# Decaying the scan's states in the copy out of PSUM, and two buffers for the inversion

## The chip, the cores and the metric

The kernel runs on one core of a Trainium2 chip. The metric is the time of one execution on the device in microseconds, as a median over several runs. The engines are TensorE (PE, with its weight loads as PEld), VectorE (DVE), ScalarE (ACT), GpSimd (POOL), and SyncE (SP), which issues the DMA transfers. Each engine works through its own queue in order.

## What is computed

The reference is a two-layer encoder. Each layer has a feed-forward half-step, a token mixer, and a second half-step, with a layer norm behind each. Layer 0 mixes by neighbourhood attention, layer 1 by a bidirectional RWKV-7 scan over 512 tokens, with 16 heads of 64 channels. The change concerns the scan alone, which in the reference reads:

```python
def step(state, inp):
    r_t, w_t, k_t, v_t, a_t, b_t = inp
    sa = jnp.einsum('zbhij,zbhj->zbhi', state, a_t)
    state = state * w_t[..., None, :] + sa[..., None] * b_t[..., None, :] + v_t[..., None] * k_t[..., None, :]
    return state, jnp.einsum('zbhij,zbhj->zbhi', state, r_t)

_, ys = lax.scan(step, jnp.zeros((2, B, H, N, N), f32), xs)
```

`z` is the direction. All of it is float32.

## The kernel before

The kernel does not step token by token. It cuts the 512 tokens into 8 chunks of 64 and takes two heads at a time, a pair; there are 8 pairs. Partitions 0 to 63 and 64 to 127 (`HALF`) hold the two directions or the two heads. For each pair there is preparation work and then a chain of 8 steps, one per chunk, in which the state of a chunk is made from that of the one before.

Preparation of a pair, by name of its function:

- `load` and `front` make the decayed a~, r~ (tile `ar`) and b~, k~ (tile `bk`) of each direction. The decay over a whole chunk is kept twice: `pe`, and `pc` with the two heads side by side.
- `grams` multiplies `bk` with `ar` for each chunk (PE, bank `g`), masks the products into `xs` (DVE), copies blocks of them to `qd` and `qc` (ACT), and has SP write parts to `az` and `xs`. At its end it multiplies `bk` by `pe`, L1067.
- `tails` transposes `bk` on PE and copies it into `tb`.
- `turn` makes `pd`, a diagonal matrix of the chunk decays for every chunk and head, L1114, and lays the values `v` out in `vt`.
- `invert` inverts the 32 x 32 triangular blocks. A DVE transpose (L1135) makes `qs` from `qd`, a DMA (L1137) sets `zs` to unit matrices, and POOL does 31 pairs of a product (L1143) and a sum (L1145). `inverted` transposes `zs` back (L1155), writes the blocks into `az` by eight DMAs (L1160), and transposes once more (L1162), into the memory of `qs`. `merge` combines the blocks on PE (L1174, L1181) and ACT.

The chain (`chain`) does for each step: products of `xs` with the state `vt` (L1202 and L1206), an ACT copy to `wr` (L1203), products with the inverse in `az` (L1215), two ACT copies into `vt` (L1216, L1217), and then the next state in bank `m`: the diagonal `pd` times the old state (L1212) plus `tb` times `vt` (L1221). Two DVE copies (L1223), one per direction, bring it to `vt` of the next chunk. `outputs` adds products to the pair's result, and `finish` and `gate` normalise and gate it.

The order on PE, ACT and DVE is written out by hand: `slot(n)` runs the chain of pair n beside the preparation of pairs n+1 to n+3 and the finish of pair n-1, and the string `SEQ[n]` says which thread goes on next, each up to its next `yield`. There c is the chain, k `inverted`, i `invert`, j `merge`, g0 and g1 `grams`, f0 and f1 `front`, t0 and t1 `tails`, n `turn`, x `finish`, e `gate`, v `values`, b `bonus`, d `outputs`, l `load`. Slots -2 and -1 have only preparation (and the thread r, projections that are computed on the side); slots 1 to 5 use the string of slot 0; slots 6 and 7 have their own, with the thread o (part of the output projection). POOL's and SP's queues follow the order in which the instructions are written. A tile's buffers are given again in turn, and a new use waits for the last readers of the buffer; `zs`, `qs` and `tm` have one, `qd`, `qc`, `ar`, `bk`, `vt` have two.

Of the kernel before, what the change touches and what calls it, by code (L numbers as in the profile page):

```python
# [10 lines left out]
F32 = mybir.dt.float32  # L11
# [3 lines left out]
AF = mybir.ActivationFunctionType  # L15
# [42 lines left out]
}  # L58
SEQ = {
# [782 lines left out]
class Scan:  # L842


    def __init__(self, k, pool, dram, consts, a2, w_r, w_v, w_out):
        self.k, self.nc, self.pool, self.dram, self.a2, self.w_r, self.w_v, self.w_out = k, k.nc, pool, dram, a2, w_r, w_v, w_out
        nc = self.nc
        self.tri = pool.tile([P, 2, P], F32, name="tri")
        self.mask = pool.tile([P, 2, 2, CH], F32, name="mask")
        self.onesb = pool.tile([P, P], F32, name="onesb")  # L850
        self.eye = consts["eye"]
        self.ah = pool.tile([P, 2, S], F32R, name="ah")
        self.xv = pool.tile([P, ND, S], F32, name="xv")
        self.consts = consts
        self.units = [(pool.tile([P, 2, 4, 2, CH], F32, name=f"xs{i}"), pool.tile([P, 2, 4, CH], F32, name=f"tb{i}"))
                      for i in range(NBUF)]


        self.az = [pool.tile([P, 2, NU, CH], F32, name=f"az{i}") for i in range(3)]
        self.eye64 = pool.tile([P, CH], F32, name="eye64")  # L860
        nc.vector.tensor_tensor(self.eye64, k.ident[:, A], k.ident[:, B], ALU.add)
        for i in range(2):
            self.clear(i)
        self.free = list(range(NBUF))
        self.taken, self.st, self.py = {}, {}, {}
# [57 lines left out]
    def run(self):  # L923
        with self.k.tc.manual_schedule(engines=MANUAL_SCAN):
            raw = self.tile("e", [P, S], 2)
            for dst, src in ((raw, self.dram["ah"]), (self.tri, self.consts["tri"])):
                self.nc.sync.dma_start(dst, src)
            list(self.load(0))
            self.k.split(self.ah[:, 0, :], self.ah[:, 1, :], raw)
            list(self.front(0, 0))  # L930
            for n in ("mask", "onesb"):
                self.nc.sync.dma_start(getattr(self, n), self.consts[n])
            self.rs, self.out = self.receptances(), self.outs()
            for n in range(-2, HEADS // 2):
                self.slot(n)
            list(self.finish(HEADS // 2 - 1))
            list(self.gate(HEADS // 2 - 1))
# [18 lines left out]
    def load(self, hp):  # L956

        k, nc, tile_ = self.k, self.nc, self.tile
        p = self.st[hp] = Pair()
        p.k, p.iv = (tile_(n, [P, S], 2) for n in ("k", "iv"))  # L960
        nc.sync.dma_start(p.k, self.dram["rkv"][1][:, hp, :])
        for h in range(2):
            nc.sync.dma_start(p.iv[HALF[h]], self.dram["iv"][2 * hp + h : 2 * hp + h + 1, :].broadcast_to([CH, S]))
        raw = tile_("a2r", [P, 2, P])
        nc.sync.dma_start(raw, self.a2[:, :, hp * P : (hp + 1) * P])
        yield
        p.a2u = self.pool.tile([P, 2, 2, P], F32R, name="a2u", tag="a2u", bufs=1)
        k.split(p.a2u[:, 0], p.a2u[:, 1], raw)
        p.pc = tile_("pc", [P, NC, 2], 4)
        p.qd = tile_("qd", [P, NU, 32], 2)  # L970
        p.qc = tile_("qc", [P, NU, 32], 2)
        p.az = self.az[hp % 3]
        p.units, p.ar, p.bk, p.pe = [], [], [], []
        yield

    def front(self, hp, z):
# [31 lines left out]
        nc.vector.scalar_tensor_tensor(a1, k1, k.col(C_NKK, hp), e1, ALU.mult, ALU.mult)  # L1008
        nc.vector.tensor_scalar(a0, k0, k.col(C_NKK, hp), None, ALU.mult)
        end = 0 if z else CH - 1  # L1010
        pe = tile_("pe", [P, NC, 1], 3)
        ends = ec[:, way, end : end + 1]
        nc.scalar.activation(pe, ends, AF.Copy)
        for h in range(2):
            nc.scalar.activation(p.pc[HALF[z], :, h : h + 1], ends[HALF[h]], AF.Copy)
        yield
# [10 lines left out]
        nc.vector.scalar_tensor_tensor(bt, chunks(th), 1.0, chunks(e2), ALU.add, ALU.mult)  # L1027
        p.ar.append(ar)
        p.bk.append(bk)
        p.pe.append(pe)  # L1030
        if z:
            yield
            nc.vector.tensor_tensor(kz, p.kz, kz, ALU.add)
# [3 lines left out]
    def grams(self, hp, z):  # L1037

        k, nc = self.k, self.nc
        p = self.st[hp]  # L1040
        ar, bk = p.ar[z], p.bk[z]
        own, other, r = HALF[z], HALF[1 - z], z * CH
        for q in range(2):
            x, az = self.take(hp, z, q)[0], p.az[:, :, z * NC + q * 4 : z * NC + q * 4 + 4]
            ss, us = slice(q * 4, q * 4 + 4), slice(z * NC + q * 4, z * NC + q * 4 + 4)
            pgs = [k.bank("g") for _ in HALF]

            for j in range(4):
                for h, hs in enumerate(HALF):
                    nc.tensor.matmul(pgs[h][:, j * P : (j + 1) * P], flat(bk[hs, q * 4 + j]), flat(ar[hs, q * 4 + j]),  # L1050
                                     start=True, stop=True)

            mask = self.mask[:, z].rearrange("p (o a) t -> p o a t", o=1).broadcast_to([P, 4, 2, CH])
            for h in range(2):
                nc.vector.tensor_tensor(x[:, h], pgs[h].rearrange("p (u a t) -> p u a t", u=4, a=2), mask, ALU.mult)
            yield
            for h, hs in enumerate(HALF):
                for d in range(2):
                    nc.scalar.activation(p.qd[h * 64 + d * 32 : h * 64 + d * 32 + 32, us, :],
                                         x[r + d * 32 : r + d * 32 + 32, h, :, 0, d * 32 : d * 32 + 32], AF.Copy)  # L1060
                nc.scalar.activation(p.qc[h * 64 : h * 64 + 32, us, :], x[r : r + 32, h, :, 0, 32:64], AF.Copy)
                nc.sync.dma_start(az[own, h], x[own, h, :, 1, :])
                nc.sync.dma_start(x[own, h], ar[hs, ss])
                yield

        bke = bk.rearrange("p s a t -> p s (a t)")
        nc.vector.tensor_tensor(bke, bke, p.pe[z].broadcast_to([P, NC, 2 * CH]), ALU.mult)  # L1067
        yield

    def tails(self, hp, z):  # L1070

# [37 lines left out]
    def turn(self, hp):  # L1109

        k, nc, tile_ = self.k, self.nc, self.tile
        p = self.st[hp]
        p.pd = tile_("pd", [P, NC, 2, CH], 2)
        nc.vector.tensor_tensor(p.pd, self.eye64.rearrange("p (a b t) -> p a b t", a=1, b=1).broadcast_to([P, NC, 2, CH]),  # L1114
                                p.pc.rearrange("p s (h o) -> p s h o", o=1).broadcast_to([P, NC, 2, CH]), ALU.mult)
        p.vt = tile_("vt", [P, NC, 2, 2, CH], 2)
        for z, zs in enumerate(HALF):
            nc.vector.memset(p.vt[zs, 0, z], 0.0)
# [3 lines left out]
        for z in range(2):  # L1122
# [4 lines left out]
                nc.scalar.activation(p.vt[HALF[1 - z], j::2, z], pv[HALF[j]].rearrange("p (t h i) -> p t h i", t=NT, h=2), AF.Copy)  # L1127
            yield

    def invert(self, hp):  # L1130

        nc, tile_ = self.nc, self.tile
        p = self.st[hp]
        qs = tile_("qs", [P, 32, 32])
        nc.vector.transpose(flat(qs), p.qd.rearrange("p u (t o) -> p t u o", o=1).broadcast_to([P, 32, NU, 2]))  # L1135
        zs = tile_("zs", [P, 32, 16])
        nc.sync.dma_start(zs, self.eye)  # L1137
        for s in range(31, 0, -1):
            c0 = s // 2
            n = 16 - c0  # L1140
# [8 lines left out]
    def inverted(self, hp):  # L1149
# [6 lines left out]
        for h in range(2):  # L1156
            for d in range(2):
                for z in range(2):
                    r, us = HALF[1 - z].start + d * 32, slice(z * NC, z * NC + NC)
                    nc.sync.dma_start(p.az[r : r + 32, h, us, d * 32 : d * 32 + 32], p.zc[h * 64 + d * 32 : h * 64 + d * 32 + 32, us])  # L1160
        yield
        nc.vector.transpose(flat(p.zt), flat(p.zc))  # L1162
        yield
# [24 lines left out]
    def chain(self, hp):  # L1188
# [6 lines left out]
        for s in range(NC):  # L1195
# [11 lines left out]
            yield  # L1207
            if 0 < s < NC - 1:

                for z, h in zh:  # L1210
                    zs = HALF[z]
                    nc.tensor.matmul(pm[zs, h], p.pd[zs, s, h], vt[zs, s, z, h], start=h == 0, stop=False)  # L1212
            for z, h in zh:
                ws = HALF[1 - z]
                nc.tensor.matmul(pw[HALF[z], 1, h], az[z][ws, h, s, :], wr[ws, h], start=True, stop=True)  # L1215
# [3 lines left out]
            if s < NC - 1:  # L1219
                for z, h in zh:  # L1220
                    nc.tensor.matmul(pm[HALF[z], h], tb[z][:, h, s % 4, :], vt[:, s, z, h], start=s + h == 0, stop=h == 1)  # L1221
                for z, zs in enumerate(HALF):
                    nc.vector.tensor_copy(vt[zs, s + 1, z], pm[zs])  # L1223
                yield

    def outputs(self, hp):
# [230 lines left out]
```

## Time and profile before

| | us |
|---|---|
| median of 3 runs | 2376.36 (2374.26 to 2377.40) |
| profiled execution, its own time | 2376.21 |
| its span, first to last instruction | 2374.3 |
| PE busy / DVE busy / ACT busy / POOL busy | 2215.5 / 1141.9 / 984.1 / 1439.5 |

Busy time counts each moment once in which an instruction of the engine is in flight. PE's busy time is an upper view: matmul records overlap. A float32 matmul appears as two records. The scan lies between about 1493 and 1960 us of the span; the rest is projections, attention and feed-forward work that the change does not touch.

### The profile page before, as it was taken

The numbers are of one execution on the slowest core, as the hardware profiler recorded it, in microseconds if no ns is written. First come the engines' busy times: TensorE is split into PE (matmuls) and PEld (weight loads), VectorE is DVE, ScalarE is ACT, GpSimd is POOL, SyncE is SP. The second block draws the span as 40 slices with busy tenths as digits, with TensorE's granted clock in tenths as the row PEclk, the third lists the DMA queues.
The fourth block names the chain that finished last, engine by engine and source line by source line (L and its number), as shares of the span: only waits on it lengthen the run. The fifth ranks groups of instructions, "written<-read, shape, count | busy, mean of one in ns | idle before, by whom it ended". The sixth has DMA issues, their size and how long they took to land.

```text
span 2374.3 us, 34996 instructions
## 1 busy us (share of the span) xinstructions
PE 2215.5 (93%) x13664; PEld 1746.6 (74%) x13664; DVE 1141.9 (48%) x1575; ACT 984.1 (41%) x1728; POOL 1439.5 (61%) x1231
## 2 busy tenths in 40 slices
PE   8999999999999999999999789799998884999998
PEld 7888878777888888888888665456666553888886
DVE  2333366355523335723335696346877546233336
ACT  3333344466433333533333435346676423233334
POOL 7787744544658785778775433136756605477863
PEclk9999999999999999999999889799999996999999
DMA  6444453421534446344445325843443516344453
GB/s 201 146 146 139 133 186 116 134 74 49 168 98 139 144 136 232 112 134 143 141 139 193 118 82 188 266 126 103 115 120 100 155 60 212 98 139 145 146 172 116
DMA packets 351361, 330.38 MB, mean 139 GB/s; under 512 B 48554, under 2 KB 277546, under 8 KB 351196
## 3 DMA queue, kind: packets, MB, share of 16 engines
q1 hardware_dynamic: 351196, 328.15, 43.9%
q8 instruction: 107, 1.75, 0.3%
q14 instruction: 58, 0.48, 0.1%
HBM read 263.05 MB, written 48.53 MB: 131 GB/s over the span
## 4 chain that ended last, share of the span: by engine, by line
PE 74%; DVE 12%; DMA 5%; issue 3%; POOL 3%; ACT 2%; SPq 1%; DVEq 0%; ACTq 0%; POOLq 0%
PE bank L201 15%; PE bank L203 15%; PE bank L202 15%; PE bank L668 12%; PE bank L239 3%; DVE x L306 2%; PE a L1091 1%; DVE x L373 1%; POOL zs L1145 1%; POOL tm L1143 1%; DVE tmp L303 1%; DVE w L197 1%; PE y L904 1%; PE g L1263 1%; PE bank L793 1%
## 5 line engine op out<-in xcount | busy, mean ns | idle before, releaser
L197 POOL TENSOR_TENSOR w<-raw,w 128x1024 fp32r<-128x1024 f32 (+2 forms) x203 | 502.4, 2475 | 319.6 <-ACT w L196 319.5
L201 PE MATMUL bank<-xT,w 128*128 128x512 f32 x1416 | 554.0, 392 | 0.0
L202 PE MATMUL bank<-xT,w 128*128 128x512 f32 x1416 | 552.0, 390 | 0.0
L203 PE MATMUL bank<-xT,w 128*128 128x512 f32 x1416 | 551.8, 390 | 0.0
L196 ACT ACTIVATE w<-raw 128x1024 fp32r<-128x1024 f32 (+1 forms) x207 | 218.7, 1057 | 339.2 <-POOL ts L639 141.9
L347 DVE SCALAR_TENSOR_TENSOR ar<-bank,tmp 128x512 f32<-128x512 f32 x88 | 60.9, 692 | 587.3 <-PE bank L203 572.4
L201 PEld LDWEIGHTS bank<-xT,w 128*128 128x128 f32 x1416 | 266.2, 188 | 55.8
L203 PEld LDWEIGHTS bank<-xT,w 128*128 128x128 f32 x1416 | 266.4, 188 | 55.5
L202 PEld LDWEIGHTS bank<-xT,w 128*128 128x128 f32 x1416 | 266.5, 188 | 54.4
L668 PE MATMUL bank<-w,ring 128*128 128x512 f32 x864 | 202.8, 393 | 11.1 <-DVE w L197 10.2
L668 PEld LDWEIGHTS bank<-w,ring 128*128 128x128 f32 x864 | 162.6, 189 | 48.6 <-DVE w L197 13.2
L1143 POOL TENSOR_TENSOR tm<-qs,zs 128x126 f32<-128x126 f32 (+22 forms) x248 | 105.0, 424 | 138.6 <-DMA zs<-in_eye_dram 85.3
L668 PE MATMUL bank<-wx,an 128*128 128x512 f32 x792 | 187.3, 389 | 0.0
L668 PEld LDWEIGHTS bank<-wx,an 128*128 128x128 f32 x792 | 148.7, 188 | 30.9
L197 POOL TENSOR_TENSOR wx<-ra,wx 128x512 fp32r<-128x512 f32 x132 | 168.3, 1302 | 0.0
L197 DVE TENSOR_TENSOR ring<-ar,ring 128x1024 fp32r<-128x1024 f32 x44 | 130.7, 2970 | 72.8 <-ACT ring L196 72.7
L345 ACT ACTIVATE tmp<-bank 128x512 f32<-128x512 f32 x88 | 52.6, 597 | 238.0 <-PE bank L203 238.0
L1145 POOL TENSOR_TENSOR zs<-zs,tm 128x126 f32<-128x126 f32 (+22 forms) x248 | 114.3, 461 | 19.4
L196 ACT ACTIVATE wx<-ra 128x512 fp32r<-128x512 f32 x132 | 83.1, 632 | 91.5 <-PE bank L668 68.0
L197 POOL TENSOR_TENSOR w<-late,w 128x1024 fp32r<-128x1024 f32 x28 | 70.2, 2507 | 79.3 <-ACT w L196 72.4
L639 POOL TENSOR_TENSOR ts<-ra 128x512 f32<-128x512 f32 x44 | 57.7, 1311 | 87.5 <-DMA raw<-in_rw_out_dram 78.5
L201 PE MATMUL bank<-xT,ring 128*128 128x256 f32 (+1 forms) x352 | 102.2, 305 | 8.6 <-ACT xT L196 6.4
(280 smaller groups left out, 3886.7 us busy)
## 6 DMA issues: line engine op xcount, KB each, us to landing
raw<-in_ffn_w_in_dram SPq DMA_DIRECT2D x176, 512.0 KB, 3.7
ra<-in_ffn_w_out_dram SPq DMA_DIRECT2D x44, 1024.0 KB, 4.9
late<-d_late SPq DMA_DIRECT2D x30, 512.0 KB, 5.3
late<-in_ffn_w_out_dram SPq DMA_DIRECT2D x28, 512.0 KB, 4.3
raw<-in_w_qkv_dram SPq DMA_DIRECT2D x24, 512.0 KB, 3.7
d_late<-ts SPq DMA_DIRECT2D x44, 256.0 KB, 3.3
d_late<-ra SPq DMA_DIRECT2D x44, 256.0 KB, 2.0
xs<-ar SPq DMA_DIRECT2D x64, 128.0 KB, 2.3
```

The source lines that it names most:

```text
L196: self.nc.scalar.activation(h, raw, AF.Copy)
L197: (eng or self.nc.vector).tensor_tensor(l, raw, h.bitcast(F32), ALU.subtract)
L201: nc.tensor.matmul(out, wh, xh, start=start, stop=False)
L202: nc.tensor.matmul(out, wh, xl, start=False, stop=False)
L203: nc.tensor.matmul(out, wl, xh, start=False, stop=stop)
L239: nc.tensor.matmul(acc[t, h], a, u[:, i, h * 512 : (h + 1) * 512], start=first and n == 0, stop=last and n == 2)
L345: nc.scalar.activation(s, pg, AF.Silu)
L347: nc.vector.scalar_tensor_tensor(raw[:, 3:7:3] if j else raw[:, 0:8:7], halves_of(pu), 0.5, halves_of(s), ALU.mult, ALU.mult)
L639: nc.gpsimd.tensor_tensor(t3, r[:, 1, 1], r[:, 0, 1], ALU.subtract)
L668: self.nc.tensor.matmul(acc, lhs, u[:, i], start=bool(first) and m == 0, stop=last and m == 2, skip_group_check=more)
L1143: nc.gpsimd.tensor_tensor(tv, qs[:, s, 0:s].rearrange("p (a o) -> p a o", o=1).broadcast_to([P, s, n]), zs[:, s : s + 1, c0:].broadcast_to ...
L1145: nc.gpsimd.tensor_tensor(zs[:, 0:s, c0:], zs[:, 0:s, c0:], tv, ALU.add)
```

## The change

The diff has three parts. The first: b~ and k~ and the old state are no longer decayed one by one. `pe`, `pd` and the unit matrix `eye64` go; the old state is added to bank `m` by a product with the unit matrix, for both heads in one instruction; and the copy of `m` to the next state becomes a product with `pc`, a number per partition and head.

The second: `qs` and `zs` have two buffers, and the unit matrices are loaded by `unit`, twice before the slots and then from `inverted` for the pair two further on.

The third: the strings of slots -2, -1 and 0 are new.

```diff
 SEQ = {
...
-    0: "f1 n x x c c c n c g0 f1 c x c d c g0 f1 v f1 c g0 g0 c c d v c f1 v l x c v f1 v c c g0 x c d l f0 x c g1 e "
...
+    0: "c f1 x f1 v c n c f1 f1 v c g0 c c d f1 c n c d g0 l v c c g0 c x f1 g0 c x x v n x t0 v c c l c d g0 f0 c "
...
-        self.eye64 = pool.tile([P, CH], F32, name="eye64")
-        nc.vector.tensor_tensor(self.eye64, k.ident[:, A], k.ident[:, B], ALU.add)
...
+            self.zs = []
+            for _ in range(2):
+                self.unit()
...
-        pe = tile_("pe", [P, NC, 1], 3)
         ends = ec[:, way, end : end + 1]
-        nc.scalar.activation(pe, ends, AF.Copy)
...
-        bke = bk.rearrange("p s a t -> p s (a t)")
-        nc.vector.tensor_tensor(bke, bke, p.pe[z].broadcast_to([P, NC, 2 * CH]), ALU.mult)
-        yield
...
-        p.pd = tile_("pd", [P, NC, 2, CH], 2)
-        nc.vector.tensor_tensor(p.pd, self.eye64.rearrange("p (a b t) -> p a b t", a=1, b=1).broadcast_to([P, NC, 2, CH]),
-                                p.pc.rearrange("p s (h o) -> p s h o", o=1).broadcast_to([P, NC, 2, CH]), ALU.mult)
...
+    def unit(self):
+        self.zs.append(self.tile("zs", [P, 32, 16], 2))
+        self.nc.sync.dma_start(self.zs[-1], self.eye)
+
...
-        qs = tile_("qs", [P, 32, 32])
+        qs = tile_("qs", [P, 32, 32], 2)
...
-        zs = tile_("zs", [P, 32, 16])
-        nc.sync.dma_start(zs, self.eye)
+        zs = self.zs.pop(0)
...
+        if hp + 2 < HEADS // 2:
+            self.unit()
         yield
...
-                for z, h in zh:
-                    zs = HALF[z]
-                    nc.tensor.matmul(pm[zs, h], p.pd[zs, s, h], vt[zs, s, z, h], start=h == 0, stop=False)
+                for z, zs in enumerate(HALF):
+                    nc.tensor.matmul(pm[zs], k.ident[zs, zs], vt[zs, s, z], start=True, stop=False)
...
-                    nc.vector.tensor_copy(vt[zs, s + 1, z], pm[zs])
+                    nc.vector.tensor_tensor(vt[zs, s + 1, z], pm[zs], p.pc[zs, s].rearrange("p (h o) -> p h o", o=1).broadcast_to([CH, 2, CH]),
+                                            ALU.mult)
```

How the instructions move on DVE, in a steady slot, from the last state copy ahead of the three transposes. Before the change (`vt<-m` is the state's copy, `qd<-zs` and the first `qs<-qd` belong to `inverted`, the second `qs<-qd` to `invert`, `bk` and `e` to `front`, `bon` to `bonus`):

```order
L1223 COPY vt<-m 64x128 x2
L1008 SCALAR_TENSOR_TENSOR ar<-k,cols,e 128x8x63
L1009 TENSOR_SCALAR ar<-k,cols 128x8
L1155 STREAM_TRANSPOSE qd<-zs 128x16x16x2
L1162 STREAM_TRANSPOSE qs<-qd 128x512
L1135 STREAM_TRANSPOSE qs<-qd 128x1024
L1017 TENSOR_TENSOR ar<-r,e 128x8x64
L1019 SCALAR_TENSOR_TENSOR iv<-k,cols,iv 128x512
L1067 TENSOR_TENSOR bk<-bk,pe 128x1024
L1223 COPY vt<-m 64x128 x2
```

The same place after the change:

```order
L1218 TENSOR_TENSOR vt<-m,pc 64x128 x2
L1149 STREAM_TRANSPOSE qd<-zs 128x16x16x2
L1158 STREAM_TRANSPOSE qs<-qd 128x512
L1130 STREAM_TRANSPOSE qs<-qd 128x1024
L1094 SCALAR_TENSOR_TENSOR kz<-r,cols,kz 128x512
L1218 TENSOR_TENSOR vt<-m,pc 64x128 x2
```

Between the two state copies stand four instructions instead of eight; the two `qs<-qd` follow one another as before, but write different buffers now.

On DVE again, the rows that follow, up to the first state copy of the next slot. Before (`pd` is the diagonal, `sm` and `yt` belong to `finish`):

```order
L1105 TENSOR_TENSOR bon<-a,v 128x512
L1023 TENSOR_TENSOR kz<-kz,k 128x512
L1024 TENSOR_TENSOR bk<-kz,e_13349 128x8x64
L1026 TENSOR_TENSOR e_13349<-iv,e_13349 128x512
L1027 SCALAR_TENSOR_TENSOR bk<-th,e_13349 128x8x64
L1114 TENSOR_TENSOR pd<-eye_10778,pc 128x1024
L1118 MEMSET vt 64x128 x2
L1281 TENSOR_REDUCE sm<-yt 128x8
```

After the change, behind the state copy that ends the rows shown above:

```order
L1009 SCALAR_TENSOR_TENSOR ar<-k,cols,e 128x8x63
L1010 TENSOR_SCALAR ar<-k,cols 128x8
L1016 TENSOR_TENSOR ar<-r,e 128x8x64
L1018 SCALAR_TENSOR_TENSOR iv<-k,cols,iv 128x512
L1022 TENSOR_TENSOR kz<-kz,k 128x512
L1023 TENSOR_TENSOR bk<-kz,e_13293 128x8x64
L1025 TENSOR_TENSOR e_13293<-iv,e_13293 128x512
L1026 SCALAR_TENSOR_TENSOR bk<-th,e_13293 128x8x64
L1099 TENSOR_TENSOR bon<-a,v 128x512
L1109 MEMSET vt 64x128 x2
```

The whole front of one direction now stands here, the diagonal is gone, and the reduction of `finish` has left this stretch: it comes after the second state copy of the slot.

## Rows read from the trace of the kernel before

**Rows 1.** Busy table by stretches of the scan; (x) counts, then clock, DMA
```profile
core 0: us, PE busy (x) PEld busy (x) DVE busy (x) ACT busy (x) POOL busy (x), PEclk, DMA share, GB/s
1493.00:1610.60 117.60, 97.53 (x509) 53.94 (x508) 50.13 (x77) 48.07 (x118) 36.76 (x93) 0.87 0.63 190
1610.60:1649.30 38.70, 37.83 (x619) 27.13 (x618) 28.42 (x50) 28.41 (x80) 18.90 (x40) 1.00 0.47 126
...
1694.20:1738.80 44.60, 40.15 (x623) 29.08 (x622) 34.94 (x68) 29.31 (x82) 29.36 (x64) 0.92 0.43 116
...
1872.00:1921.70 49.70, 44.53 (x556) 24.28 (x554) 15.65 (x41) 14.29 (x39) 22.57 (x62) 0.97 0.30 95
```

**Rows 2.** Waits: engine, line, waited for, us in total, times, longest us
```profile
POOL tm L1143 <- DMA zs<-in_eye_dram: 85.3, 5, 37.2
```

**Rows 3.** Chain that ended last, 1682 to 1694: start us, us, what
```profile
1682.46 1.08 DVE qd L1155
...
1689.89 3.36 DMA zs<-in_eye_dram
...
1693.42 0.55 POOL tm L1143
```

**Rows 4.** Timeline of DVE and POOL: start us, us, instruction, [idle before it <-releaser]
```profile
1683.57 0.71 DVE L1162 STREAM_TRANSPOSE qs<-qd 128x512 f32<-128x512 f32 x1
1685.72 1.25 DVE L1135 STREAM_TRANSPOSE qs<-qd 128x1024 f32<-128x1024 f32 x1 [1.44 <-PE p L1174]
...
1693.42 0.54 POOL L1143 TENSOR_TENSOR tm<-qs,zs 128x31 f32<-128x31 f32 x1 [10.99 <-DMA zs<-in_eye_dram]
1693.78 1.26 DVE L1114 TENSOR_TENSOR pd<-eye,pc 128x1024 f32<-128x1024 f32 x1
1694.03 1.13 POOL L1145 TENSOR_TENSOR zs<-zs,tm 128x31 f32<-128x31 f32 x1
...
1695.55 0.26 POOL L1145 TENSOR_TENSOR zs<-zs,tm 128x30 f32<-128x30 f32 x1
```

**Rows 5.** Busy table by stretches, two inversions from first to last instruction
```profile
1693.40:1727.20 33.80, 29.80 (x390) 21.64 (x388) 25.91 (x55) 19.66 (x59) 29.00 (x62) 0.90 0.42 118
1876.10:1903.40 27.30, 24.76 (x252) 13.13 (x253) 8.13 (x25) 6.81 (x19) 22.52 (x62) 0.94 0.32 116
```

**Rows 6.** Groups by line, 1493 to 1960: busy us, mean ns | idle before
```profile
L1055 DVE TENSOR_TENSOR xs<-g,mask 128x512 f32<-128x512 f32 x64 | 41.2, 686 | 18.4 <-PE g L1050 17.8
...
L1223 DVE COPY vt<-m 64x128 f32<-64x128 f32 x112 | 32.2, 288 | 60.0 <-PE m L1221 57.2
...
L1067 DVE TENSOR_TENSOR bk<-bk,pe 128x1024 f32<-128x1024 f32 x16 | 20.3, 1270 | 0.0
...
L1114 DVE TENSOR_TENSOR pd<-eye,pc 128x1024 f32<-128x1024 f32 x8 | 9.9, 1244 | 0.0
...
L182 DVE TENSOR_TENSOR sm<-sm 128x8 f32<-128x8 f32 x24 | 5.0, 208 | 0.8
```

**Rows 7.** Chain that ended last, 1719 to 1762: start us, us, what
```profile
1719.74 0.38 PE m L1212 x8
...
1740.07 0.70 DVE sm L1281
1740.79 0.18 DVE sm L1282
1741.00 0.77 DVE yt L1283
1741.79 0.63 ACT yh L1285
...
1742.64 0.81 PE c L1215 x7
...
1745.12 2.06 PE g L1050 x16
...
1760.99 1.09 PE g L1050 x16
```

More of the change, by code (lines that the diff above doesn't have):

```diff
@@ L972, in load @@
         p.az = self.az[hp % 3]
-        p.units, p.ar, p.bk, p.pe = [], [], [], []
+        p.units, p.ar, p.bk = [], [], []
         yield
@@ L1029, in front @@
         p.bk.append(bk)
-        p.pe.append(pe)
         if z:
```

12 rows, old and new, of the table SEQ are left out of this document.

## Prediction

> **What bounds the kernel now.** I read the busy table by stretches of the scan first, then the list of waits, then the chain that ended last, then single stretches of the timeline. The scan works on eight head pairs in slots; a slot is taken from the first state matmul (L1202) of one pair to that of the next. The startup before slot 0 takes 117.6 us, slot 0 38.7 us, slot 2 44.6 us, and slots 1 to 5 together 1872.0 - 1649.3 = 222.7 us, 44.5 us each [rows 1]. No engine fills a steady slot: DVE is busy 34.9 of 44.6 us, ACT 29.3, POOL 29.4, and PE's records cover 40.2 us but overlap, at a mean granted clock of only 0.92 of full speed [rows 1]; PE has slack. What fills the slot must be loops of dependent work, and I see two of nearly the same length.
>
> The first is POOL's. The inversion of a pair runs from 1693.4 to 1727.2, 33.8 us [rows 5]. Then POOL stands still: the next one starts only when a fresh unit matrix has landed, which is the longest sum among POOL's waits, 85.3 us in five cases [rows 2]. In the chain one sees why: the single buffer is free when DVE has transposed it (from 1682.46), its reload is issued behind eight other writes, takes 3.36 us from 1689.89, and POOL goes on at 1693.42 [rows 3], idle for 10.99 us [rows 4]. 33.8 + 11.0 is 44.8 us, a slot.
>
> The second loop is that of the engines that work in order: the order puts some fifteen wide DVE instructions from the transposes to the first state copy of the next slot, the longest such stretch. The chain there goes through the first part of the previous pair's normalisation (0.70, 0.18 and 0.77 us on DVE), a 0.63 us square on ACT, and only then ACT can copy the step's product, for which PE's L1215 waits (1742.64) [rows 7]. PE idles meanwhile, and what it does next runs at 1.2 GHz: sixteen L1050 records take 2.06 us there and 1.09 us at 2.4 GHz later in the slot [rows 7].
>
> **The change, part by part.**
>
> The unit matrix. With two buffers and a load issued when the previous pair's inversion is read, a whole slot ahead, the load leaves POOL's loop. A second buffer of the other tile, qs, lets the transpose that starts an inversion (L1135, now L1130) follow directly on the two that end the one before; until now it waited for PE's L1174, which read the same buffer (1.44 us) [rows 4]. What is left between two inversions is three transposes one behind the other, 1.08 + 0.71 + 1.25 us [rows 3, 4], and about 0.3 us each way between the engines: 3.6 us instead of 11. DVE's wait for POOL stands where it stood; behind it are queued the transposes, step 6's state copy and the next front, and PE's L1170 waits for the second transpose, so what POOL is late, all of them are late.
>
> POOL's speed. The inversion took 27.3 us where DVE was busy 8.1 us of it and 33.8 us where DVE was busy 25.9 us [rows 5]. The rows show why: one POOL instruction took 1.13 us while DVE's L1114 ran, and its like took 0.26 us just after [rows 4]. L1114 reads two SBUF tiles, as L1067 does. Both go: three instructions per slot, 2 x 1.27 + 1.24 = 3.8 us [rows 6]. If each holds POOL for about two thirds of its length where it meets an inversion, that is some 1.3 us of 33.8; but of the 11 us in which DVE worked without disturbing POOL only 3.6 us are left, which gives most of that back. I take 33.5 us. POOL's loop is then 33.5 + 3.6 = 37.1 us, a floor for the steady slot.
>
> DVE's removed work. Sixteen L1067 (20.3 us) and eight L1114 (9.9 us) leave DVE [rows 6]. All of L1114 and one of a slot's two L1067 stand in that long stretch; the other stands ahead of a state copy. So the loop of the in-order engines loses up to 3.8 us: 44.5 - 3.8 = 40.7 us. The new order also puts the normalisation's first part behind step 1's state copy, so that 0.70 + 0.18 + 0.77 + 0.63 = 2.3 us go from the first step [rows 7]; ACT has a few copies and exponentials there in exchange, so I count half: 39.5 us. PE's stretch at 1.2 GHz costs up to 1 us per sixteen such records [rows 7] and may go with the stall; I count 0.5 us: 39.0 us. That is above POOL's floor, so I take 39.0 us for slots 1 to 5, with 37.1 and 42.5 as ends (the latter if only half of the 3.8 us is on the path).
>
> The state's copy. It becomes a product with the decay, read from PSUM and a broadcast column: 112 instructions, 14 in a slot, two on the path of each step. The copy takes 0.288 us [rows 6]. No row has the new form; the nearest are the product out of PSUM with 512 columns (0.686 us) and a product of 8 columns (0.208 us) [rows 6]. A straight line between them gives 0.322 us for 128 columns, 0.034 more. The ends are 0.208 (below the copy, -9.0 us over 112) and 0.686 us (+44.6 us). I take the line: 112 x 0.034 = 3.8 us, of which I count 1.4 us, since in steady slots it lies beside POOL's loop and only in three of eight slots (0, 6, 7) nothing of POOL binds.
> The Trainium skill (VectorE: DVE Perf Modes, The perf-mode tier table) gives a copy out of PSUM up to twice the rate of a product of two tensors. By that rule and the page's own cycles the product would be an estimated 64 / 0.96 = 67 ns dearer, 7.5 us in all and 3.7 us above the sum below; the trace speaks against a copy at twice the rate, as the line between two product rows comes within 0.034 us of it.
>
> PE. Four 64-column products with the diagonal per step (0.38 us for eight records [rows 7]) become two of 128 columns with the unit matrix. Two such products are four records, a quarter of L1050's sixteen in 1.09 us [rows 7], 0.27 us. It is 0.1 us in 48 steps, 5 us if PE were on the path; PE has slack, so nothing, with -5 as the end below. ACT loses sixteen tiny copies: nothing, as ACT isn't full. The transposes of b~ and k~ no longer wait for L1067, which is in the 3.8 us.
>
> Queues. SP issues as many unit loads as before; two of them move to the start, ahead of the projections' loads. In the worst case they delay them by 2 x 3.36 us [rows 3]; PE has the second front's matmuls in front of those, so I take 0, with +4. The startup loses two L1067 per pair on DVE too: -4 at best. Slots 6 and 7 keep their order and are mostly PE's; the last inversion starts earlier, and the tails end earlier: I take -1.5 us, from 0 to -5.
>
> The sum: slots 1 to 5, 222.7 - 5 x 39.0 = 27.7 us gained; slot 0, which has no normalisation to move, half of its 3.8 us, 1.9 us; the end 1.5 us; the state's product costs 1.4 us; startup 0. Together 29.7 us. The profiled execution took 2376.21 us (its span and 1.9 us around it), 0.15 us from the median of the runs. The forecast is 2376.2 - 29.7 = 2346.5 us.
>
> **Rivals.**
>
> 1. The in-order loop hardly shortens: the new order trades one stall for another (on ACT, step 0 now has the y copy, two exponentials and a reversal between the two copies of the chain). Then the steady slot is 41 to 43 us: 222.7 - 5 x 42 = 12.7 us, with the rest of the sum about 14.7 us gained, 2361 us (2356 to 2369). For it: both loops are equal now, so freeing one alone gives nothing. Against: most of the removed DVE work stands in DVE's longest stretch.
>
> 2. POOL's floor is reached, and startup and end give their best: 222.7 - 5 x 37.1 = 37.2 us, with slot 0, the startup and the end some 43 us, 2333 us (2328 to 2338). For it: slot 0, with the work that goes still in it and no normalisation, ran in 38.7 us [rows 1]. Against: every wait would have to fall into place.
>
> 3. POOL is held for the whole of every DVE instruction with two SBUF inputs. By the code eighteen wide ones remain in a steady slot, 13.9 us at the 0.77 us of the normalisation's [rows 7]. Inversion and all of these in a row give 27.3 + 13.9 + 3.6 = 44.8 us, the slot of now, and the time stays at 2376 us within 5. For it: L1145's 1.13 us beside L1114. Against: with all of them in a slot of 44.5 us the inversion took 33.8 us, so the hold is partial.
> The Trainium skill (GPSIMD Engine Reference, Specifications) states that GpSimd shares its SBUF interfaces with VectorE and that instructions with two SBUF inputs contend; the trace agrees in the kind, and its sizes decide how much.
>
> 4. Slower: the product in the state's copy. It stands twice in each step on the only path from one state to the next, so each nanosecond more of the 112 is paid in full where the chain binds. Without it the sum gains 31.1 us, so it decides from 0.288 + 31.1 / 112 = 0.57 us on; at the upper end, 0.686 us, the kernel would take 2376.2 - 31.1 + 44.6 = 2390 us. For it: no row has this form, a column broadcast along 64. Against: L1055 broadcasts its mask too and the line gives 0.322 us.
>
> That the change doesn't do what it says (the load still late behind SP's writes) would be rival 1 with more, since a load a slot ahead has some 30 us to spare.
>
> **Chances.** Forecast (2338 to 2356) 0.60, rival 1 0.19, rival 2 0.12, rival 3 0.04, rival 4 0.05. The range that leaves out no more than 2 in 10 runs from 2331 to 2365 us; nearly all of the chance is on one side. A change of 0.2%, 4.8 us, is about what a measurement of this kernel can tell from none. Faster by more: 0.60 + 0.19 + 0.12 = 0.91; within: rival 3, 0.04; slower: 0.05.
>
> **What would show it.** In the changed profile POOL's wait for the unit matrix is gone from the waits, the gap between inversions is 3.5 to 4.5 us, and the inversion takes 33 to 34.5 us. Steady slots are 38 to 40 us, PE's mean clock in them is above 0.92, and the state's product takes 0.29 to 0.33 us. I am wrong if POOL shows gaps of over 6 us while the slots stay above 41 us (the in-order loop binds), if the inversion takes over 37 us (contention), or if the state's product takes over 0.4 us.

## The result and the profile after

The changed kernel takes 2356.44 us, the median of five runs (2352.33 to 2363.28); the kernel before took 2374.49 us beside it (2373.00 to 2377.40). The ratio is 0.9927 [0.9906, 0.9948], a gain of 18 us where 29.7 were forecast. The profiled execution of the changed kernel is one of its longer ones, 2361.35 us with a span of 2359.5 us, so that the two spans differ by 14.8 us only.

The busy table of the changed kernel, by the stretches of [rows 1] and, in its last two rows, of [rows 5]:

```profile
core 0: us, PE busy (x) PEld busy (x) DVE busy (x) ACT busy (x) POOL busy (x), PEclk, DMA share, GB/s
1493.00:1612.40 119.40, 100.72 (x524) 57.30 (x522) 40.64 (x65) 50.66 (x118) 28.55 (x70) 0.89 0.64 197
1612.40:1655.70 43.30, 39.88 (x593) 28.40 (x592) 27.75 (x52) 27.83 (x77) 34.21 (x78) 0.92 0.41 112
1693.90:1732.70 38.80, 37.68 (x600) 26.89 (x596) 31.68 (x65) 29.09 (x80) 28.48 (x63) 1.00 0.50 136
1848.70:1899.30 50.60, 44.74 (x532) 24.45 (x530) 15.79 (x41) 14.16 (x39) 17.29 (x46) 0.93 0.29 90
1686.50:1719.70 33.20, 32.14 (x518) 23.18 (x513) 26.94 (x58) 25.13 (x68) 28.42 (x62) 1.00 0.46 127
1841.70:1869.50 27.80, 21.94 (x316) 12.71 (x310) 8.40 (x27) 10.32 (x27) 22.98 (x62) 0.88 0.51 151
```

The third row is a steady slot: 38.8 us instead of 44.6, at the full clock instead of 0.92. Slots 1 to 5 together run from 1655.7 to 1848.7, 193.0 us, 38.6 each. The first two rows are longer than before, though: the startup by 1.8 us and slot 0 by 4.6 us. The account of the two spans is +1.8 (startup), +4.6 (slot 0), -29.7 (slots 1 to 5), +0.9 (slot 6) and +7.6 us from slot 7's start to the end of the kernel, -14.8 in all.

POOL's waits in the scan, which answer to [rows 2]:

```profile
engine line waited for: us in total, times, longest us
POOL tm L1137 <- DVE qs L1130: 64.3, 2, 48.9
POOL tm L1137 <- issue: 31.1, 6, 7.2
```

The unit matrix is gone from them. Between two inversions POOL now stands still for 3.1 to 7.2 us, six times; the two long waits are the first two inversions, which wait for their transpose. The timeline of DVE and POOL between two inversions of a steady slot answers to [rows 3, 4]:

```profile
1678.66 0.67 POOL L1139 TENSOR_TENSOR zs<-zs,tm 128x16 f32<-128x16 f32 x1
...
1682.43 0.61 DVE L1218 TENSOR_TENSOR vt<-m,pc 64x128 f32<-64x128 f32 x2 [0.50 <-PE m L1216]
1683.07 1.06 DVE L1149 STREAM_TRANSPOSE qd<-zs 128x512 f32<-128x512 f32 x1
1684.16 0.71 DVE L1158 STREAM_TRANSPOSE qs<-qd 128x512 f32<-128x512 f32 x1
1685.12 1.25 DVE L1130 STREAM_TRANSPOSE qs<-qd 128x1024 f32<-128x1024 f32 x1 [0.24 <-ACT qd L1057]
...
1686.49 0.60 POOL L1137 TENSOR_TENSOR tm<-qs,zs 128x31 f32<-128x31 f32 x1 [7.17 <-issue]
```

POOL is done at 1679.3, but DVE comes to its transpose only at 1683.07, behind work of its own and a wait of 0.50 us for a product of the chain, and finds it ready. So POOL is not what binds in this slot. The groups that answer to [rows 6]:

```profile
L1053 DVE TENSOR_TENSOR xs<-g,mask 128x512 f32<-128x512 f32 x64 | 41.2, 686 | 27.9 <-PE g L1048 27.6
L1218 DVE TENSOR_TENSOR vt<-m,pc 64x128 f32<-64x128 f32 x112 | 32.2, 287 | 50.5 <-PE m L1216 48.6
L1207 PE MATMUL m<-vt,ident 64*64 64x128 f32 x192 | 20.4, 290 | 0.0
```

The state's product takes 287 ns, the copy took 288. The last view is the chain in the same slot, for [rows 7]:

```profile
1697.63 1.10 PE a L1085 x2
1698.73 0.38 PE m L1216 x8
1699.11 1.14 PE g L1048 x16
...
1703.61 0.70 DVE sm L1277
1704.33 0.18 DVE sm L1278
1704.54 0.91 DVE yt L1279
```

The normalisation's first part stands behind a state copy of a later step, as the order says, and still on the chain; the sixteen records that took 2.06 us at half the clock take 1.14.

### The profile page after: what moved, and what is told of

Same layout as the page of the kernel before. It is cut to its first block, busy times and chain, and to the rows that moved or that the text cites. A ratio compares the mean times of both kernels' runs of the same rounds, so it can differ in the third digit from the quotient of the medians.

```text
span 2359.5 us, 34563 instructions
## 1 busy us (share of the span) xinstructions
PE 2206.3 (94%) x13472; PEld 1740.2 (74%) x13472; DVE 1113.7 (47%) x1550; ACT 983.4 (42%) x1712; POOL 1438.0 (61%) x1231
## 5 line engine op out<-in xcount | busy, mean ns | idle before, releaser
L668 PEld LDWEIGHTS bank<-wx,an 128*128 128x128 f32 x792 | 148.6, 188 | 30.9
```

Of the source, the lines that this page charges most:

```text
L668: self.nc.tensor.matmul(acc, lhs, u[:, i], start=bool(first) and m == 0, stop=last and m == 2, skip_group_check=more)
```

## Experiments

Each kernel ran beside the kernel before; that one's medians were 2375.8 to 2376.7 us. "Steps" are the times from a step's first chain product to that of the next, in a steady slot; before they are 8.28, 5.22, 6.12, 5.25, 4.03, 4.96 and 6.85 us.

**e1_unit_only.** The kernel before, with the unit matrices two pairs ahead and nothing else (`qs` stays single).

```diff
-        zs = tile_("zs", [P, 32, 16])
-        nc.sync.dma_start(zs, self.eye)
+        zs = self.zs.pop(0)
...
+        if hp + 2 < HEADS // 2:
+            self.unit()
```

> The kernel before, with only the unit matrix in two buffers and loaded two pairs ahead; decays, the other tile's single buffer and the order as before. Two equal loops (my theory): POOL's idle time between inversions falls from 11 us to some 5 us, but the in-order loop keeps the steady slot at 44 to 44.5 us: 0 to 5 us faster than before (2370 to 2375 us), and DVE's first transpose no longer waits for POOL. POOL's loop alone binds (rival): the slot falls to about 39 us, 2348 us.

Measured: 2374.55 us, ratio 0.9991 [0.9979, 1.0002], steady slot 44.2 us. The inversions start earlier and take 35.0 to 35.5 us, and POOL still stands idle for 8.1 to 10.2 us between them, not for the 5 us that I expected. Taking the load out of POOL's loop gives nothing by itself, as two equal loops demand.

**e2_decay_only.** The kernel before, with the states decayed in the copy and the old state added by the unit matrix: L1067, L1114, `pe` and `eye64` gone, in the old order.

```diff
-        nc.vector.tensor_tensor(bke, bke, p.pe[z].broadcast_to([P, NC, 2 * CH]), ALU.mult)
...
-                    nc.vector.tensor_copy(vt[zs, s + 1, z], pm[zs])
+                    nc.vector.tensor_tensor(vt[zs, s + 1, z], pm[zs], p.pc[zs, s].rearrange("p (h o) -> p h o", o=1).broadcast_to([CH, 2, CH]),
+                                            ALU.mult)
```

> The kernel before, with only the decay moved into the copy out of PSUM (no decayed b~, k~, no diagonal); one buffer for the unit matrix and the order as before. Two equal loops: POOL's loop of 33.5 + 11 us stays, the steady slot is 43.5 to 44.5 us, 2368 to 2375 us. In-order loop alone binds (rival): the slot falls to some 40.7 us, 2356 us.

Measured: 2369.10 us, 0.9969 [0.9956, 0.9982], steady slot 43.6 us, inversions 30.9 to 31.8 us. DVE has 3.8 us less to do in a slot, and the slot loses 1.0; step 0 falls to between 5.7 and 7.3 us. In slots 2 and 3 every other step stays within 0.1 us, but in slots 1 and 5 step 2 grows from 6.1 to 7.7 us, and in slot 4 step 6 takes 7.8 us. Slot 0 takes 38.5 us instead of 38.7.

**e3_both_old_order.** The changed kernel with the three old strings.

```diff
-    0: "c f1 x f1 v c n c f1 f1 v c g0 c c d f1 c n c d g0 l v c c g0 c x f1 g0 c x x v n x t0 v c c l c d g0 f0 c "
...
+    0: "f1 n x x c c c n c g0 f1 c x c d c g0 f1 v f1 c g0 g0 c c d v c f1 v l x c v f1 v c c g0 x c d l f0 x c g1 e "
...
```

> The changed kernel with the order strings of before, so both parts without the third. Two equal loops: the in-order loop is shorter by the 3.8 us of DVE work and POOL's by its load, the steady slot is 40 to 41.5 us, and startup and slot 0 are not later than before: 2350 to 2358 us. The order does it (rival): the slot stays at 43 us or more, 2366 us or more.

Measured: 2372.09 us, 0.998 [0.9969, 0.9991], steady slot 44.2 us. My theory missed by 14 us or more, and the rival that the order does it was right: both loops are relieved, and the slot is shorter by 0.3 us only. The busy table of a slot, and the chain through its step 2:

```profile
1690.00:1733.70 43.70, 39.70 (x599) 27.63 (x598) 31.23 (x64) 29.04 (x80) 27.72 (x64) 0.96 0.43 115
```

```profile
1701.10 0.71 PE c L1198 x7
...
1702.49 1.73 PE a L1085 x2
1704.22 0.31 PE m L1207
...
1704.86 1.71 PE a L1085 x2
1706.57 0.38 PE m L1216 x8
1706.95 1.91 PE a L1085 x4
1708.86 0.38 PE c L1198 x8
```

Step 0 is 5.8 to 7.4 us now, but step 2 has grown from 6.1 to 7.7 in four of five slots. The old string puts eight records of the projection of the values (L1085) between the chain's products of this one step, and PE works in order: 1.73 + 1.71 + 1.91 us. In the kernel before the same products stood at the same place and took 1.06 + 1.06 + 1.91 us, so the queue did not change; the clock did. Step 2 by the busy table, here and in the kernel before:

```profile
1701.10:1708.80 7.70, 7.70 (x54) 3.36 (x54) 5.94 (x15) 1.61 (x6) 6.60 (x15) 0.78 0.27 69
```

```profile
1707.70:1713.80 6.10, 6.10 (x56) 2.94 (x56) 5.77 (x15) 2.10 (x7) 5.32 (x11) 1.00 0.33 89
```

PE is busy through the whole step in both. Just ahead of it PE waits for DVE's state copy, in e3 and in the kernel before:

```profile
1701.10 0.71 PE L1198 MATMUL c<-vt,xs 128*64 128x64 f32 x7 [1.40 <-DVE vt L1218]
```

```profile
1707.68 0.71 PE L1202 MATMUL c<-vt,xs 128*64 128x64 f32 x7 [0.96 <-DVE vt L1223]
```

Behind the idle 1.40 us a part of e3's step ran at 1.2 GHz, half the full clock; behind the 0.96 us none did. In the one slot of e3 whose step 2 ran at the full clock, it takes 6.1 us as before, and steps 0 and 1 have the lower clock. Over slots 1 to 5 the granted clock is 0.93 in the kernel before and 0.93 here. So what step 0 won by the removed DVE work is taken back in part by a stretch at the lower clock in another step. Why the clock falls at one step and not at another was not tested.

**e4_old_start.** The changed kernel with the old strings of slots -2 and -1 and the new one of the steady slots.

```diff
-    -2: "g0 v f1 f1 f1 f1 f1 f1 g0 l g0 r r g0 g0 v r g1 g1 g1 v r g1 v g1 g1 v t0 r g0 r r v f1 b r r t0 v r l v t1 "
...
+    -2: "v f1 g0 f1 f1 r f1 g0 v f1 g0 l r f1 f1 g0 r g0 g0 g0 g1 r g1 b t0 r g1 g1 r g1 g1 g1 i t0 v l r t1 r t1 r v "
...
```

> The changed kernel with the order strings of the two startup slots taken from before; the steady string is the new one. If the new startup order is what makes slot 0 start 1.8 us and end 6.4 us later than before (the first inversion starts at 1554 us instead of 1536, the second at 1611 instead of 1600, and slot 0 waits for it), slot 0 falls from 43.3 to 38 to 39 us and the kernel is 5 to 8 us faster than the changed one, 2348 to 2352 us. If the two unit loads at the start or the removed work are the reason (rival), the inversions start as late as in the changed kernel and the time is the same, 2356 us.

Measured: **2341.45 us** (2338.74 to 2344.03), 0.9849 [0.9831, 0.9866], faster than both kernels. Startup, slot 0 and a steady slot:

```profile
1493.00:1606.00 113.00, 98.05 (x513) 54.48 (x511) 43.40 (x69) 50.17 (x118) 33.73 (x84) 0.88 0.68 210
1606.00:1643.50 37.50, 37.04 (x593) 26.31 (x592) 24.72 (x47) 27.77 (x77) 26.11 (x60) 1.00 0.42 111
1681.80:1720.80 39.00, 37.72 (x600) 26.89 (x596) 31.44 (x65) 29.14 (x80) 28.70 (x63) 1.00 0.49 134
```

That is 15.0 us less than the changed kernel, where I had expected 5 to 8. From e3 to e4 only the steady string differs, and slots 1 to 5 go from 44.2 to 38.3 us each: the order is worth some 30 us here. A part of this is the clock, which is 1.00 in e4 through all of slots 1 to 5. As an estimate from e3's steps, a stretch at the lower clock costs 1.2 to 1.6 us (step 0 at 7.0 to 7.4 instead of 5.8, step 2 at 7.7 instead of 6.1), and e3 has eight such stretches in five slots, some 11 of the 30 us. From the changed kernel to e4 only the startup's strings differ, and slot 1 starts at 1643.5 instead of 1655.7. The reason is in two stretches of the changed kernel's timeline, in slots -2 and 0:

```profile
1552.91 1.24 DVE L1130 STREAM_TRANSPOSE qs<-qd 128x1024 f32<-128x1024 f32 x1
...
1554.28 0.24 POOL L1137 TENSOR_TENSOR tm<-qs,zs 128x31 f32<-128x31 f32 x1 [48.94 <-DVE qs L1130]
...
1643.15 1.04 DVE L1149 STREAM_TRANSPOSE qd<-zs 128x512 f32<-128x512 f32 x1 [3.11 <-POOL zs L1139]
```

The new strings put the transpose of the first inversion later: POOL starts at 1554.3 and, for the second, at 1611.5, in e4 at 1539.1 and 1599.3, in the kernel before at 1536.0 and 1599.6. In slot 0 DVE, and with it the chain, then waits for the second inversion's end.

**e5_one_unit.** e4 with one `zs`, loaded in `invert` as before.

```diff
-        zs = self.zs.pop(0)
+        zs = tile_("zs", [P, 32, 16])
+        nc.sync.dma_start(zs, self.eye)
```

> The changed kernel with the startup order of before (as in the run on the startup order, 2341.5 us), and with one buffer for the unit matrix again, loaded where an inversion begins. If POOL's loop matters in the new order, POOL idles some 11 us between inversions again, the steady slot is 33.6 + 11 = 44 to 45 us and the kernel some 30 us slower, 2370 us. If the order of PE's queue alone makes the short slot (rival), it stays at 38 to 39.5 us and the time within 5 us of 2341.5.

Measured: 2360.05 us, 0.9932 [0.9905, 0.9958], steady slot 42.8 us. The timeline between two inversions:

```profile
1671.61 0.22 POOL L1137 TENSOR_TENSOR zs<-zs,tm 128x16 f32<-128x16 f32 x1
1671.86 1.04 DVE L1147 STREAM_TRANSPOSE qd<-zs 128x512 f32<-128x512 f32 x1 [4.28 <-POOL zs L1137]
...
1683.48 0.24 POOL L1135 TENSOR_TENSOR tm<-qs,zs 128x31 f32<-128x31 f32 x1 [11.65 <-DVE bon L1096]
```

POOL stands still for 11.65 us again, DVE waits 4.28 us for it, and the slot follows POOL. In the new order the load ahead of time is worth 4.5 us per slot, 18.6 us in all; in the old one it was worth nothing. I had expected slots of 44 to 45 us. They are shorter since the inversion takes only 31 us; DVE is busy 21.6 us within one here, 26.7 in e4, so my reading, not tested by itself, is that more of DVE's work falls into POOL's pause.

**e6_two_sbuf and e7_psum.** e4 with DVE work added, 3.9 and 4.1 us per slot: in e6 products by 1.0 of two SBUF tiles, in e7 six of a slot's eight masking products (my text for e7 calls them sixteen) done twice, which read PSUM and one SBUF tile.

```diff
+                    nc.vector.tensor_tensor(bke, bke, self.ones.broadcast_to([P, NC, 2 * CH]), ALU.mult)
...
+        for _ in range(2):
+            nc.vector.tensor_tensor(chunks(p.v), chunks(p.v), self.ones.broadcast_to([P, NC, CH]), ALU.mult)
```

```diff
-            for h in range(2):
+            for h in (0, 0, 1) if z == q == 0 else (0, 0, 1, 1) if q else (0, 1, 1):
```

> The changed kernel with the startup order of before, and with as much DVE work as the change took away put back as products with 1.0 that read two SBUF tiles: one of 128x1024 at the end of each grams, two of 128x512 in turn, 3.9 us per slot. As I predicted (DVE on the loop of the in-order engines): the slot grows by 3 to 4 us, to 42 us, the kernel to 2356 to 2364 us. Rival from the runs so far (that work lies beside PE's queue): the slot grows by 0 to 1.5 us, 2342 to 2350 us. If POOL is held as well, the inversion grows from 33.7 to some 35 us.

> The changed kernel with the startup order of before, and with six of the sixteen masking products in a slot done twice, 4.1 us of DVE work per slot that reads PSUM and one SBUF tile. If DVE's time alone counts, the same as the run with products that read two SBUF tiles, within 3 us. If holding POOL counts, the inversion stays at 33.7 us here and the kernel is 3 us or more faster than that run.

Measured: e6 2355.40 us, 0.9905 [0.988, 0.9929], slot 39.6 us; e7 2359.08 us, 0.9926 [0.9905, 0.9946], slot 40.9 us. One steady inversion in e4, in e6 and in e7, from first to last instruction:

```profile
1674.40:1707.80 33.40, 32.18 (x520) 23.22 (x517) 26.70 (x58) 25.13 (x68) 28.62 (x62) 1.00 0.47 128
```

```profile
1676.70:1712.30 35.60, 34.06 (x487) 24.23 (x486) 31.17 (x65) 26.30 (x71) 30.75 (x62) 1.00 0.52 138
```

```profile
1681.00:1713.70 32.70, 30.16 (x468) 21.40 (x462) 27.14 (x57) 22.54 (x61) 27.89 (x62) 1.00 0.45 127
```

And DVE's wait for POOL in e6:

```profile
DVE qd L1156 <- POOL zs L1146: 9.7, 6, 3.6
```

Two SBUF inputs lengthen the inversion by some 2 us (33.4 to 34.2 us in the steady slots of e4, 35.3 to 35.7 in e6) and make DVE wait for POOL in every slot: 35.5 us and a gap of 4.2 are the slot. It grows by 1.3 us, as the rival had it, and not by the 3 to 4 that I predicted; the kernel's time lies between the two ranges. In e7 the steady inversions take 32.7 to 33.4 us, but this alone proves little: the rows above show 0.4 us more of DVE's work within e7's inversion than within e4's, and 4.5 more within e6's, as most of the doubled masks fall into POOL's pause. Single instructions settle it. In e4, POOL beside a mask product out of PSUM (`xs<-g,mask`) and beside products of two SBUF tiles:

```profile
1688.41 1.29 DVE L1053 TENSOR_TENSOR xs<-g,mask 128x512 f32<-128x512 f32 x2 [0.47 <-PE g L1048]
1689.26 0.41 POOL L1137 TENSOR_TENSOR tm<-qs,zs 128x126 f32<-128x126 f32 x1
1689.61 0.68 DVE L1022 TENSOR_TENSOR kz<-kz,k 128x512 f32<-128x512 f32 x1
1689.74 0.84 POOL L1139 TENSOR_TENSOR zs<-zs,tm 128x126 f32<-128x126 f32 x1
...
1694.40 0.82 DVE L1026 SCALAR_TENSOR_TENSOR bk<-th,e 128x512 f32<-128x512 f32 x1
1694.75 0.75 POOL L1137 TENSOR_TENSOR tm<-qs,zs 128x126 f32<-128x126 f32 x1
1695.25 1.29 DVE L1053 TENSOR_TENSOR xs<-g,mask 128x512 f32<-128x512 f32 x2
1695.58 0.43 POOL L1139 TENSOR_TENSOR zs<-zs,tm 128x126 f32<-128x126 f32 x1
```

The same two POOL instructions take 0.41 and 0.43 us beside the masks and 0.75 and 0.84 us beside the others. So reading PSUM leaves POOL alone. That part of the theory held; the forecast that e7 would then be the faster one by 3 us or more did not. Its masks stand ahead of state copies on DVE, and the steps that hold them grow: 6.85, 5.15 and 5.28 us where e4 has 5.55, 4.4 and 4.69. What DVE's work costs depends on where it stands.

**e8_order_only.** The kernel before with the new steady string, as far as its tiles allow: `i` behind the second `j`, since `qs` is single, and `t0` behind the last `g0`, since `tails` needs the decayed `bk`.

```diff
-    0: "f1 n x x c c c n c g0 f1 c x c d c g0 f1 v f1 c g0 g0 c c d v c f1 v l x c v f1 v c c g0 x c d l f0 x c g1 e "
...
+    0: "c f1 x f1 v c n c f1 f1 v c g0 c c d f1 c n c d g0 l v c c g0 c x f1 g0 c x x v n x v c c l c d g0 "
...
```

> The kernel before, decays and single buffers kept, with the new steady string as far as it can be had: the inversion's start stands behind the second piece of merge, since they share a buffer, the first tails stand behind the last grams, since b~ and k~ are decayed there, and grams have their seventh piece. If the new order needs the other two parts (POOL's loop: inversion 33.8 us, some 10 us from one inversion's end to the next one's start in the order, and 4 us for the load), the steady slot is 47 to 49 us and the kernel slower than before, 2385 to 2400 us. If the order alone makes the short slot (rival), the slot is 38 to 41 us, 2345 to 2360 us.

Measured: 2404.50 us, 1.012 [1.0095, 1.0145], slot 50.5 us, slower than before and than expected. The waits in two slots:

```profile
PE g L1076 <- DVE bk L1066: 15.3, 4, 4.0
```

PE waits four times, 3.8 us each, for the decay of `bk`, with the chain queued behind it; steps 3 and 5 take 10 to 11 us, and the clock of a slot is 0.87. As this run places the decay, the new order cannot stand with it; another place for it was not tried. DVE waits for POOL 0.6 us in these two slots, so POOL's loop is not what binds here.

**e9_spread_v, e10_x_later, e11_ij.** Single moves of the new string in e3, each added to the one before: the v pieces spread over the steps; the x pieces (`finish`) as in the new string; `i` directly behind `k`.

```diff
-    0: "f1 n x x c c c n c g0 f1 c x c d c g0 f1 v f1 c g0 g0 c c d v c f1 v l x c v f1 v c c g0 x c d l f0 x c g1 e "
+    0: "f1 n x x c v c c n v c g0 f1 c x c d c g0 f1 f1 c g0 g0 v c c d c f1 l x c f1 v v c c g0 x c d l f0 "
...
+    0: "f1 n c v x c c n v c g0 f1 c c d c g0 f1 f1 c g0 g0 v c c d c f1 l x c f1 v v x x x c c g0 c d l f0 "
...
+       "c g1 g1 x c g1 c c d g0 f0 g0 v e c f1 g1 c c b c d g1 g1 t0 c t0 n f0 v v c k k i c d j v c f0 g1 c b f0 d f0 c c j c t1 t1 d",
```

> The changed kernel with the order strings of before (2372.1 us, steady slot 44.2 us), except that the nine pieces of the value projection are spread over the steady slot as in the new string. If matmuls of that projection on the chain's way through PE's queue make the old slot long (8.3 us of the chain of one slot there, 2.8 us in the new order), steps 1 and 2 shorten from 5.2 and 6.1 to 7.7 us to some 4.4 and 5.5 us and the slot to 41 to 42 us: 2357 to 2362 us. If other waits take their place (rival), the slot stays at 43 us or more, 2366 us or more.

> The changed kernel with the old order, the value projection spread (2365.0 us, steady slot 43.0 us, step 0 of it 6.5 to 9.4 us), and the pieces of finish placed as in the new string, so that the normalisation's first part no longer stands ahead of step 0's second half. As I predicted, 2.3 us leave step 0: it falls to 5.5 to 6.5 us, the slot to 41 us and the kernel to 2353 to 2358 us. If another wait takes its place (rival), step 0 shrinks but the slot stays at 42.5 us or more, 2362 us or more.

> The run before in this list, and in addition the inversion's start directly behind the last one's transposes and the second piece of merge one step later, as in the new string. If merge's second matmuls ahead of step 6's state make that step long (6.5 us, 4.3 us in the new order), step 6 falls to 4.3 to 5 us and the last step grows by 1 to 1.5 us; the slot is 1 to 2 us shorter than in the run before, some 39.5 to 40.5 us, 2346 to 2352 us. If other waits take their place (rival), the slot does not move by more than 0.5 us.

Measured: 2364.97 us, 0.995 [0.9931, 0.997]; 2369.51 us, 0.9974 [0.996, 0.9988]; 2373.46 us, 0.9995 [0.9977, 1.0013]. Slots 43.0, 44.2 and 44.5 us. Each move shortens the step it is meant for: step 2 from 7.7 to 4.7, step 0 from 6.5 to 9.4 us down to 5.0, step 6 only from 6.5 to 6.4. Each time other steps grow: in e9 step 0 from between 5.8 and 7.4 to between 6.5 and 9.4, steps 4 and 5 to 4.7 and 5.8; in e10 step 4 to between 7.5 and 8.1, with a granted clock of 0.58 to 0.78 in it; in e11 the last step from 3.9 to 5.5. So e9 gains some 7 us against e3, and the two moves after it lose that again; the slots of e10 and e11 are those of the rivals named for them. None of these three pieces, added in this sequence, holds the 30 us; which pieces of the string do stays open. The clock alone does not: this slot of e11 ran at the full clock and is as long as a slot of e3:

```profile
1740.20:1784.40 44.20, 38.55 (x599) 27.28 (x598) 30.67 (x64) 29.11 (x80) 27.03 (x63) 1.00 0.43 119
```

## Why the prediction was right, and where not

**The steady slot.** 39.0 us was forecast, 38.6 measured, and most of the signs named for it came: no wait for the unit matrix, inversions of 33.1 to 34.2 us (33.5 forecast), the clock above 0.92. The gap between inversions, 3.5 to 4.5 us by forecast, was 3.1 us where DVE did wait for POOL (1643.1 to 1646.2) and 3.9 to 7.2 elsewhere, so POOL's floor was not reached. The 0.3 us each way between the engines, for which I had no row, are 0.12 us from DVE's transpose to POOL (1686.37 to 1686.49) and 0.03 from POOL to DVE (1671.83 to 1671.86 in e5). The time of the kernel, 2356.4 us, lies in the range of 2331 to 2365 but just above the forecast's own band (2338 to 2356), where rival 1 begins; the slots are the forecast's and not rival 1's 41 to 43 us, and the gain that is missing was lost outside them.

**The step that failed in it** is "So the loop of the in-order engines loses up to 3.8 us". The DVE work left, but the loop did not shorten by it: 1.0 us in e2, 0.3 in e3. I had taken the longest stretch of one engine for the whole loop; in the old order a stretch of PE at half its clock moved into step 2, and rival 1's mechanism (one stall traded for another) is what the kernel does there. The number came out by luck: two errors met. The new string, which I priced at 1.2 us for the normalisation and 0.5 for the clock, is worth about 6 us per slot, some 2 of them the clock by the estimate above. The two other parts are its conditions: without the preload it loses 4.5 us per slot (e5), and with the decay of `bk`, as e8 places it, it is slower than before. Put back in the new order, 3.9 to 4.1 us of DVE's work cost 1.3 us per slot through POOL (e6) or 2.6 through the state copies (e7), so the removal is worth more there than in the old order. I had followed the chain through the first step only, and not the clock of each step.

**Startup and slot 0.** Forecast 0 and -1.9 us, measured +1.8 and +4.6. I priced two loads and two removed instructions there and did not follow the two new strings: they start the first inversion 18 us and the second 12 us later than the kernel before. e4 shows that this is their doing; of the sum's errors it is the largest to which a run gives a cause, and of the opposite sign.

**Slot 6 and the end.** Forecast -1.5 us; slot 6 gained nothing (+0.9). From slot 7's start to the end of the kernel only the state's product in slot 7's chain differs, and that chain takes 38.3 us in both. In the thirteen profiled executions of this study the whole stretch took 452.6 (before) to 460.2 us (after), so the two profiles shown are its two ends. The 7.6 us lie in the last part, behind the scan, where the code is the same: 314.3 us before and 321.9 after, both at a granted clock of 0.99. What makes them differ I did not settle.

**The state's product.** Forecast +1.4 us, measured 0: 287 ns against 288. Rival 4 is dead, as its price began at 570 ns. I misread the Trainium skill here: the cell of its table that I used (VectorE: DVE Perf Modes, The perf-mode tier table) is an upper bound over all types, and the same page (Why PSUM operands drop a tier) holds float32 with a PSUM operand to the single rate. The trace agrees with that, copy and product at 288 and 287 ns. The 3.7 us that I gave beside the sum is also measured from the full 3.8 us and not from the 1.4 that the sum counts.

**Contention.** Rival 3 asked for 44.8 us per slot; e6's 3.9 us lengthened the inversion by some 2. The Trainium skill (GPSIMD Engine Reference, Specifications) names two SBUF inputs as what contends; e4's trace agrees, 0.75 to 0.84 us for a POOL instruction beside such a product against 0.41 to 0.43 beside one that reads PSUM.

**PE** was taken at nothing, having slack. In the steady slot its records now cover 37.7 of 38.8 us, at the full clock. That is an upper view, as they overlap; that PE binds next is likely but not shown.

## What to carry to other kernels

Where a loop runs through engines that work in order, follow the chain through every step of it before an instruction's removal is counted, and compare the granted clock step by step: here the time won in one step was lost in part to the lower clock in another. A part that gives nothing alone (a load ahead of time, a product saved) may be the condition for an order that does, so price the parts together, and the order by its own run. Strings for the startup have to be priced too: the old ones beneath the new steady order gave a kernel of 2341.45 us, 15.0 us below the changed one.

## What the runs showed of the hardware

DVE's work held POOL by its kind: in e4 POOL instructions of 128 x 126 took 0.75 and 0.84 us beside DVE products of two SBUF tiles, and 0.41 and 0.43 us beside products that read PSUM and one SBUF tile. In e6, 3.9 us more per slot of the first kind lengthened an inversion from 33.4 to 35.6 us. The same eight PE records of a step took 4.03 us with the clock at 1.00 (before) and 5.35 with it at 0.78 over the step (e3). A DVE product of a PSUM tile with a broadcast column took as long as a plain copy (287 and 288 ns for 64 x 128).
